# FFN down product of a two-layer hybrid decoder: pairs of row blocks by seven quarter products, weight sums on GpSimd

## The chip, the cores and the metric

The kernel runs on one core of a Trainium2 chip. The metric is the device time of one execution in microseconds, the median of several runs. All arithmetic is on fp32 data; TensorE multiplies operands of type fp32r (fp32 rounded to the shorter form that TensorE takes in one pass).

## The reference, cut to what matters

The trunk has two layers. Each is a half SwiGLU FFN, a token mixing stage (retention, block attention and a convolution side by side), and another half SwiGLU FFN, all with residuals. There are thus four FFNs, and the change touches only their second product. Sequence 256, model width 1024, FFN width 2816.

```python
def swiglu(h, wg, wu, wd):
    return (jax.nn.silu(h @ wg) * (h @ wu)) @ wd
...
    for l in range(DEPTH):
        h = rms_norm(x, ffn1_norm[l])
        x = x + FFN_RES_WEIGHT * swiglu(h, ffn1_wg[l], ffn1_wu[l], ffn1_wd[l])
```

## The kernel before, in words

**Precision.** Every product of two fp32 matrices is made from halves: each operand is split into hi (ScalarE copies it into fp32r, L145 or L196) and lo (VectorE subtracts hi from the source, L146 or L197). A product is then three matmuls: hi by hi, hi by lo, lo by hi.

**The weight stream.** All weights pass once from HBM in "units", each of up to 128x2048 (1 MB). `stream_setup` (L94) lists the units in the order of their use. `fetch` (L118) issues a unit's DMA on SyncE's queue into one of three "raw" tiles (`RBUFS`). `pump` (L130) splits one half of a unit ("a piece", 128x1024) into a whi and a wlo tile; there are 10 such pairs (`WBUFS`). `take` (L152) hands pieces to the matmuls, `free` (L157) gives a pair back. `tick` (L160), called between groups of matmuls, pumps one piece if a pair is free and moves on the other chains of work.

**An FFN** (L387) has 22 row blocks j of 128 hidden columns. The first two are made by `first_pair`. Each later block is one call of `single` (L423): a gate projection and an up projection of 16 matmuls each (8 of 512 columns at L207, 8 of 256 columns at L208), the gate's in a PSUM bank of the tag "mm", the up's in one of the tag "tr", two banks each. After a projection `joined` (L210) folds the bank: ScalarE copies its upper half (L212) and VectorE adds the lower half (L213); only then may the bank be written again. SiLU (L436), the product with up (L438) and the split of the result into hi and lo follow.

**The second product.** `down` (L442) multiplies row block j (128 hidden columns, for each half t of the sequence) by the weights of its 128 rows: for each t two halves of 512 output columns and three matmuls for each, that is 12 matmuls of 512 columns for a block and 24 for a pair of blocks (L450, L451, L454). They accumulate in the four "acc" banks through the whole FFN. The loop at L459 makes two `single`s and then the `down` of the pair made two steps earlier; one such step is called a period here. The last four blocks (`TAIL`) are done at the end, bank by bank (L478), so that the residual of each bank (L484) and the next norm can start while the other banks are still being summed; the transposes of the normed rows (L354) are put between these matmuls.

**Order.** TensorE's order is the program's own throughout. The other engines are ordered by the scheduler, by priority and readiness in its own model, except where `ordered(True)` fixes the program's order (the first pair, the tail). Each engine then executes its queue strictly in that order, and waits are semaphores.

## Time and profile before

| what | value |
|---|---|
| median of 3 runs | 992.77 us (992.19 to 992.94) |
| profiled execution, its own time | 992.42 us |
| its span, first to last instruction | 990.6 us |
| mean granted TensorE clock | 0.999 of full speed |
| PE busy | 973.7 us, 98% |
| DVE (VectorE) busy | 685.4 us, 69% |
| ACT (ScalarE) busy | 537.9 us, 54% |
| POOL (GpSimd) busy | 64.5 us, 7% |

Time of an execution and span differ by 1.8 us, which lies around the first and last instruction. Busy times are unions of records; records of neighbouring instructions of one engine overlap a little, so a sum of single durations is somewhat larger than the busy time.

### The profile page before, as it was taken

The page shows a single profiled execution, that of the slowest core. Times are in us where ns is not written, and L with a number is a line of the kernel's source. Part 1 is how long each engine was busy: PE and PEld are TensorE (multiplying, and loading weights), DVE is VectorE, ACT ScalarE, POOL GpSimd, SP SyncE. Part 2 cuts the span into 40 slices and gives each one's busy share as a digit, 9 for nine tenths or more (in the row PEclk, how much of TensorE's full clock was granted, in tenths as well). Part 3 has the DMA queues.
Part 4 walks back from the last instruction along what each step waited for, and adds up shares of the span by engine and source line. Part 5 has one row for each costly group of instructions (what it writes and reads, how often), then busy time and mean ns, then how long its engine had stood idle before and what let it go on. Part 6 is the DMA issues. An engine that isn't in the chain of part 4 may idle for free.

```text
span 990.6 us, 13759 instructions
## 1 busy us (share of the span) xinstructions
PE 973.7 (98%) x5312; PEld 849.3 (86%) x5312; DVE 685.4 (69%) x1032; ACT 537.9 (54%) x904; POOL 64.5 (7%) x109
## 2 busy tenths in 40 slices
PE   6999999999999999999999999999999999999997
PEld 4888888898997888888888888888989888888885
DVE  6986566569976866666577656566799677666653
ACT  6755555366554755555465545454665456555542
POOL 1000000021141000000000000002100400000000
PEclk9999999999999999999999999999999999999999
DMA  8965554436441855555546555544545437555511
GB/s 307 341 204 202 181 198 163 144 124 215 169 175 64 298 188 194 187 196 184 198 164 222 189 190 192 185 155 138 190 145 192 144 140 264 174 207 177 204 47 43
DMA packets 28722, 180.69 MB, mean 182 GB/s; under 512 B 3440, under 2 KB 3824, under 8 KB 10480
## 3 DMA queue, kind: packets, MB, share of 16 engines
q1 hardware_dynamic: 27360, 176.07, 51.2%
q10 hardware_dynamic: 1296, 3.74, 1.1%
q8 instruction: 42, 0.69, 0.3%
q14 instruction: 24, 0.20, 0.1%
HBM read 178.74 MB, written 1.05 MB: 181 GB/s over the span
## 4 chain that ended last, share of the span: by engine, by line
PE 93%; DVE 5%; ACT 1%; DMA 1%; issue 1%; SPq 0%; POOLq 0%; POOL 0%; DVEq 0%; ACTq 0%
PE mm L207 15%; PE tr L207 15%; PE acc L451 8%; PE acc L450 8%; PE acc L454 8%; PE tr L208 8%; PE mm L208 8%; PE mm L201 4%; PE mm L202 4%; PE mm L203 4%; DVE wlo L146 2%; DVE ac L698 2%; PE acc L207 1%; PE tr L354 1%; PE acc L641 1%; PE mm L787 1%
## 5 line engine op out<-in xcount | busy, mean ns | idle before, releaser
L146 DVE TENSOR_TENSOR wlo<-raw,whi 128x1024 fp32r<-128x1024 f32 (+2 forms) x348 | 402.9, 1169 | 176.9 <-ACT whi L145 173.2
L145 ACT ACTIVATE whi<-raw 128x1024 fp32r<-128x1024 f32 (+2 forms) x348 | 348.6, 1013 | 224.8 <-PE acc L454 87.7
L207 PE MATMUL tr<-hT,whi 128*128 128x512 f32 x640 | 226.0, 391 | 0.0
L207 PE MATMUL mm<-hT,whi 128*128 128x512 f32 x640 | 225.9, 391 | 0.0
L208 PE MATMUL tr<-hT,wlo 128*128 128x256 f32 x640 | 180.5, 282 | 0.0
L208 PE MATMUL mm<-hT,wlo 128*128 128x256 f32 x640 | 180.4, 282 | 0.0
L207 PEld LDWEIGHTS mm<-hT,whi 128*128 128x128 f32 x640 | 120.1, 188 | 25.9
L207 PEld LDWEIGHTS tr<-hT,whi 128*128 128x128 f32 x640 | 120.1, 188 | 25.2 <-issue 0.2
L450 PE MATMUL acc<-whi,hf 128*128 128x512 f32 x352 | 137.7, 391 | 0.0
L451 PE MATMUL acc<-wlo,hf 128*128 128x512 f32 x352 | 137.2, 390 | 0.0
L208 PEld LDWEIGHTS mm<-hT,wlo 128*128 128x128 f32 x640 | 120.8, 189 | 1.4
L208 PEld LDWEIGHTS tr<-hT,wlo 128*128 128x128 f32 x640 | 121.0, 189 | 0.0
L454 PE MATMUL acc<-whi,hf 128*128 128x512 f32 x352 | 113.6, 389 | 0.0
L201 PE MATMUL mm<-whi,hT 128*128 128x384 f32 (+1 forms) x288 | 107.1, 372 | 0.0
L202 PE MATMUL mm<-wlo,hT 128*128 128x384 f32 (+1 forms) x288 | 101.6, 353 | 0.0
L203 PE MATMUL mm<-whi,hT 128*128 128x384 f32 (+1 forms) x288 | 101.1, 351 | 0.0
L454 PEld LDWEIGHTS acc<-whi,hf 128*128 128x128 f32 x352 | 66.1, 188 | 13.9
L450 PEld LDWEIGHTS acc<-whi,hf 128*128 128x128 f32 x352 | 66.1, 188 | 13.6
L451 PEld LDWEIGHTS acc<-wlo,hf 128*128 128x128 f32 x352 | 66.2, 188 | 12.3
L436 ACT ACTIVATE s<-part 128x256 f32<-128x256 f32 x80 | 33.2, 415 | 78.5 <-DVE part L213 78.4
L213 DVE TENSOR_TENSOR part<-part,tr 128x256 f32<-128x256 f32 x80 | 33.6, 420 | 46.8 <-ACT part L212 46.8
L201 PEld LDWEIGHTS mm<-whi,hT 128*128 128x128 f32 x288 | 54.6, 190 | 5.2 <-issue 1.3
(151 smaller groups left out, 954.6 us busy)
## 6 DMA issues: line engine op xcount, KB each, us to landing
raw<-in_wgb SPq DMA_DIRECT2D x80, 1024.0 KB, 4.9
raw<-in_wd SPq DMA_DIRECT2D x44, 1024.0 KB, 4.9
raw<-in_win SPq DMA_DIRECT2D x28, 768.0 KB, 4.5
raw<-in_wout SPq DMA_DIRECT2D x8, 1024.0 KB, 4.8
raw<-in_wga SPq DMA_DIRECT2D x6, 1024.0 KB, 5.1
raw<-in_wcv SPq DMA_DIRECT2D x4, 1024.0 KB, 4.8
raw<-in_wga SPq DMA_DIRECT2D x8, 256.0 KB, 6.5
g<-in_fgain ACTq DMA_DIRECT2D x3, 512.0 KB, 3.7
```

The costliest lines, as they stand in the source:

```text
L145: nc.scalar.activation(hi[:, c], src, AF.Copy)
L146: nc.vector.tensor_tensor(lo[:, c], src, hi[:, c].bitcast(F32), op=OP.subtract)
L201: mm(out, ah, wh, start=start, stop=False)
L202: mm(out, ah, wl, start=False, stop=False)
L203: mm(out, al, wh, start=False, stop=stop)
L207: mm(out, wh, x, start=start, stop=False)
L208: mm(out[:, :S], wl, x[:, 0], start=False, stop=stop)
L213: self.nc.vector.tensor_tensor(v, lo, ps[:, :S], op=OP.add)
L436: nc.scalar.activation(s, v, AF.Silu)
L450: mm(ys[t][h], hi[:, ts], wh[:, n], start=first, stop=False)
L451: mm(ys[t][h], hi[:, ts], wl[:, n], start=False, stop=False)
L454: mm(ys[t][h], lo[:, ts], wh[:, n], start=False, stop=last)
```

## The change

With two row blocks u = (2u, 2u+1) as the inner dimension, the two halves of the sequence as rows and the two halves of 512 output columns as columns, the product of a pair is a 2 by 2 by 2 block product: eight block products, three matmuls each. After the change the first nine pairs of an FFN (`FAST`) use Strassen's algorithm in the form with 15 sums: seven block products, with four sums of weight blocks, four sums of activation blocks and seven sums of products. The last four row blocks (`TAIL`) stay as they were.

- The four sums of weights (128x512 each) are made in place in the raw tile by GpSimd (`sums`). The unit is split in four parts instead of two pieces: B11 alone (128x512, own tiles `wh`, 2 pairs), then B21 and B22 (128x1024), then, after the sums, T1 and T2, and T3 and T4 (128x1024 each). In the stream the last two parts come after the next unit's pieces.
- The four sums of activations (128x128 each) are made by GpSimd in `paired`; the seven blocks are then split, 128x256 and 128x640, instead of 128x256 twice.
- Six of the products stay in PSUM for the FFN: four in the "acc" banks, two in the "mm" banks. So from block 6 on both projections of `single` use the two "tr" banks. The seventh (number 4) goes to a "tr" bank for each pair and is added to the residual at once by VectorE.
- `combine` forms the sums of products before the tail: one ScalarE copy, eight VectorE instructions of 128x512.
- `WBUFS` is 9, and tile pairs are given back in the order of the stream (`release`). `fetch` is held until the raw tile's earlier unit has had all its parts pumped.
- The host lays the two column halves of the down weights the other way round.

```diff
-WBUFS = 10
+FAST = (FT - TAIL) // 2
+WBUFS = 9
+HBUFS = 2
...
                 for p in range(1, FT // 2):
-                    u += [(a["wgb"][f, 2 * p - 2 + i], 2048) for i in range(2)]
+                    plain(a["wgb"][f, 2 * p - 2], 2048)
                     if p > 1:
-                        u.append((a["wd"][f, p - 2], 2048))
+                        w = add(a["wd"][f, p - 2], 2048)
+                        parts.extend(((w, "b11"), (w, "b2")))
+                    plain(a["wgb"][f, 2 * p - 1], 2048)
+                    if p > 1:
+                        parts.extend(((w, "t12"), (w, "t34")))
...
+    def sums(self, raw):
+        b11, b12, b21, b22 = [raw[:, i * 512:(i + 1) * 512] for i in range(4)]
+        gp = self.nc.gpsimd.tensor_tensor
+        gp(b11, b12, b11, op=OP.subtract)
+        gp(b12, b22, b12, op=OP.subtract)
+        gp(b22, b22, b11, op=OP.subtract)
+        gp(b21, b22, b21, op=OP.subtract)
 
     def pump(self):
...
-        while len(self.raws) < min(u + RBUFS, len(self.units)):
+        u, kind = self.parts[self.nparts]
+        half = kind == "b11"
+        if half and self.nhalves == self.half_free + HBUFS:
+            return False
+        if not half and self.nslots == self.oldest + WBUFS:
+            return False
+        while len(self.raws) < len(self.units) and len(self.raws) <= u + RBUFS - 1:
+            if len(self.raws) >= RBUFS and self.left[len(self.raws) - RBUFS]:
+                break
             self.fetch()
...
+        else:
+            if kind == "t12":
+                src = raw.rearrange("p (b n) -> p b n", b=4)[:, 0::3]
+                self.split(*[x.rearrange("p (b n) -> p b n", b=2) for x in (hi, lo)], src)
+            else:
+                first = {"b11": 0, "b2": 1024, "t34": 512}[kind]
+                self.split(hi, lo, raw[:, first:first + size])
+            if kind == "b2":
+                self.sums(raw)
+            self.quads.setdefault(u, {})[kind] = (hi, lo, self.nslots)
...
+    def release(self, seq):
+        self.freed.add(seq)
+        while self.oldest in self.freed:
+            self.oldest += 1
...
+    def free_quad(self, q):
+        self.half_free += 1
+        for k in ("b2", "t34", "t12"):
+            self.release(q[k][2])
...
+            def paired(u):
+                r = rows.pop(u)
+                a11, a12, s1, s2, s4, a21, a22 = [r[:, i] for i in range(7)]
+                gp = nc.gpsimd.tensor_tensor
+                gp(s1, a21, a22, op=OP.add)
+                gp(a21, a11, a21, op=OP.subtract)
+                gp(s2, s1, a11, op=OP.subtract)
+                gp(s4, a12, s2, op=OP.subtract)
+                last = self.scratch(F32R)
+                self.split(*[last[:, h * 256:(h + 1) * 256].rearrange("p (b s) -> p b s", b=2) for h in range(2)], r[:, 5:7])
+                five = fp.tile([P, 2, 5, P], F32R, tag="five", bufs=3, name=self.name("five"))
+                self.split(five[:, 0], five[:, 1], r[:, 0:5])
...
-                for gu, bank in enumerate((self.mmb, self.trb)):
+                for gu, bank in enumerate((self.mmb if j < 6 else self.trb, self.trb)):
...
+            def fast(u):
+                q = self.take_quad()
...
+                terms = {4: ("A22", "T4"), 1: ("A11", "B11"), 6: ("S2", "T2"), 5: ("S1", "T1"), 7: ("S3", "T3"), 3: ("S4", "B22"), 2: ("A12", "B21")}
                 mm = nc.tensor.matmul
+                for i, (x, y) in terms.items():
+                    if i == 4:
+                        bank = self.trb()
+                    else:
+                        if u == 0:
+                            P_[i] = self.mmb() if i in (3, 7) else self.acc()
+                        bank = P_[i]
...
+                    mm(bank, hi, wh, start=first, stop=False)
+                    mm(bank, hi, wl, start=False, stop=False)
+                    mm(bank, lo, wh, start=False, stop=last)
+                    if i == 4:
+                        xs = self.x[1][:, 512:]
+                        nc.vector.scalar_tensor_tensor(xs, bank, -0.5, xs, op0=OP.mult, op1=OP.add)
+                    if i in (6, 7, 2):
+                        self.tick()
+                self.free_quad(q)
...
+            def combine():
...
+                c1, u2, u4 = tmp(), tmp(), tmp()
+                nc.scalar.activation(c1, P_[1], AF.Copy)
+                nc.vector.tensor_tensor(u2, c1, P_[6], op=OP.add)
+                nc.vector.tensor_tensor(u4, u2, P_[5], op=OP.add)
+                resid(0, 0, u4)
+                resid(0, 1, c1)
+                nc.vector.tensor_tensor(u2, u2, P_[7], op=OP.add)
+                resid(1, 0, P_[5])
+                resid(1, 0, u2)
+                resid(1, 1, u2)
...
                 if p > 1:
-                    for j in (2 * p - 4, 2 * p - 3):
-                        (w,) = self.take(1)
-                        for t in range(NT):
-                            down(j, t, w)
-                            if t == 1:
-                                self.free()
-                            self.tick()
+                    fast(p - 2)
...
             tail = self.take(TAIL)
             self.ordered(True)
+            combine()
             for t in range(NT):
                 for h in range(2):
+                    bank = P_[3 - h] if t == 0 else self.acc()
                     for j in range(FT - TAIL, FT):
-                        down(j, t, tail[j - (FT - TAIL)], (h,))
+                        down(j, bank, t, tail[j - (FT - TAIL)], h, t == 1 and j == FT - TAIL)
                         self.tick()
-                    xs = self.x[t][:, h * 512:(h + 1) * 512]
-                    nc.vector.scalar_tensor_tensor(xs, ys[t][h], 0.5, xs, op0=OP.mult, op1=OP.add)
+                    resid(t, h, bank)
                     nxt.half(t, h)
```

## Rows read from the trace of the kernel before

**Rows 1.** The page, parts 1 and 4: busy times, shares of the chain.

```profile
PE 973.7 (98%) x5312; PEld 849.3 (86%) x5312; DVE 685.4 (69%) x1032; ACT 537.9 (54%) x904; POOL 64.5 (7%) x109
...
PE 93%; DVE 5%; ACT 1%; DMA 1%; issue 1%; SPq 0%; POOLq 0%; POOL 0%; DVEq 0%; ACTq 0%
```

**Rows 2.** Stretches: length, each engine's busy us (instructions), clock, DMA share, GB/s.

```profile
25.00:50.00 25.00, 25.00 (x143) 22.00 (x142) 22.59 (x32) 19.76 (x32) 0.00 (x0) 1.00 0.96 345
50.00:75.00 25.00, 25.00 (x133) 21.54 (x133) 21.33 (x55) 12.80 (x21) 0.27 (x1) 1.00 0.59 195
...
400.00:425.00 25.00, 25.00 (x132) 21.54 (x131) 14.96 (x21) 13.17 (x20) 0.00 (x0) 1.00 0.54 183
```

**Rows 3.** Timeline of SyncE's queue: start us, us, instruction; the same unit three periods apart.

```profile
396.35 0.33 SPq L125 DMA_DIRECT2D raw<-in_wd  x1
...
446.05 0.33 SPq L125 DMA_DIRECT2D raw<-in_wd  x1
```

**Rows 4.** Timeline of PE: a pair's first matmul, and the matmul behind its 24.

```profile
398.98 0.39 PE L450 MATMUL acc<-whi,hf 128*128 128x512 f32 x1
...
404.44 0.40 PE L207 MATMUL mm<-hT,whi 128*128 128x512 f32 x1
```

**Rows 5.** Groups by shape: count, busy us, mean ns, idle before and its releasers.

```profile
L146 DVE TENSOR_TENSOR wlo<-raw,whi 128x1024 fp32r<-128x1024 f32 x284 | 345.9, 1226 | 163.7 <-ACT whi L145 160.0
...
L146 DVE TENSOR_TENSOR wlo<-raw,whi 128x768 fp32r<-128x768 f32 x56 | 52.1, 949 | 13.0 <-ACT whi L145 13.0
...
L213 DVE TENSOR_TENSOR part<-part,tr 128x256 f32<-128x256 f32 x80 | 33.6, 420 | 46.8 <-ACT part L212 46.8
...
L484 DVE SCALAR_TENSOR_TENSOR x<-acc,x 128x512 f32<-128x512 f32 x16 | 11.0, 686 | 14.4 <-PE acc L454 14.4
...
L146 DVE TENSOR_TENSOR wlo<-raw,whi 128x512 fp32r<-128x512 f32 x8 | 5.2, 685 | 0.2 <-ACT whi L145 0.2
```

**Rows 6.** Timelines of POOL and DVE: sums in SBUF, beside each other and alone.

```profile
269.70 1.10 POOL L533 TENSOR_TENSOR w<-w,w 128x384 f32<-128x384 f32 x1 [6.65 <-DVE w L532]
269.85 1.23 DVE L698 SCALAR_TENSOR_TENSOR ac<-u,vec,ac 128x256 f32<-128x256 f32 x1
272.59 0.47 DVE L698 SCALAR_TENSOR_TENSOR ac<-u,vec,ac 128x256 f32<-128x256 f32 x1
...
692.39 0.40 POOL L521 TENSOR_TENSOR w<-r,r 128x96 f32<-128x96 f32 x1
```

**Rows 7.** Timelines of DVE and POOL near 688 us: four splits and a small sum.

```profile
687.62 4.09 DVE L146 TENSOR_TENSOR wlo<-raw,whi 128x768 fp32r<-128x768 f32 x4
688.67 3.29 POOL L519 TENSOR_TENSOR r<-w,pc 128x96 f32<-128x96 f32 x1 [1.79 <-ACT w L513]
```

**Rows 8.** Timeline of one `single`: the gate's last matmul, its bank's readers, the up projection.

```profile
407.11 0.28 PE L208 MATMUL mm<-hT,wlo 128*128 128x256 f32 x1
407.23 0.39 PE L207 MATMUL tr<-hT,whi 128*128 128x512 f32 x1
...
408.27 0.37 ACT L212 ACTIVATE part<-mm 128x256 f32<-128x256 f32 x1
...
409.54 0.41 DVE L213 TENSOR_TENSOR part<-part,mm 128x256 f32<-128x256 f32 x1
...
410.00 0.39 PE L207 MATMUL mm<-hT,whi 128*128 128x512 f32 x1
```

**Rows 9.** Timelines of PE and DVE in an FFN's tail, up to the first transpose.

```profile
487.27 0.39 PE L450 MATMUL acc<-whi,hf 128*128 128x512 f32 x1
...
492.91 0.69 DVE L484 SCALAR_TENSOR_TENSOR x<-acc,x 128x512 f32<-128x512 f32 x1 [1.30 <-PE acc L454]
...
495.44 0.88 DVE L348 TENSOR_SCALAR xr<-xr,r 128x512 f32<-128x512 f32 x2 [1.11 <-POOL r L344]
...
496.11 0.38 PE L354 MATMUL tr<-ident,xr 128*128 128x128 f32 x2
```

**Rows 10.** DMA issues: KB each, median us to landing.

```profile
raw<-in_wd SPq DMA_DIRECT2D x44, 1024.0 KB, 4.9
```

More of the change, by code (lines that the diff above doesn't have):

```diff
@@ L95, in stream_setup, with add, plain @@
         a = self.a
-        u = []
+        u, parts = [], []
+        def add(src, n):
+            u.append((src, n))
+            return len(u) - 1
+        def plain(src, n):
+            i = add(src, n)
+            parts.extend((i, h) for h in range(2))
         for l in range(L):
@@ L150, in pump @@
+        self.nparts += 1
+        self.left[u] -= 1
+        if half:
+            self.nhalves += 1
+        else:
+            self.nslots += 1
         return True
@@ L456, in ffn, with down @@
+            def down(j, bank, t, w, h, first):
+                hi, lo = [x[:, t * P:(t + 1) * P] for x in hf[j]]
+                wh, wl = [x[:, (1 - h) * 512:(2 - h) * 512] for x in w]
+                mm = nc.tensor.matmul
+                mm(bank, hi, wh, start=first, stop=False)
+                mm(bank, hi, wl, start=False, stop=False)
+                mm(bank, lo, wh, start=False, stop=j == FT - 1)
             first_pair()
```

145 lines of the change are left out of this document (92 added, 53 removed).

## The prediction

> **What bounds the kernel now.** I read the page first. TensorE is busy for 98% of the span and holds 93% of the chain of waits [rows 1], so the kernel is bound by TensorE. An edit gains only what it takes off TensorE's queue, and loses whatever makes TensorE wait. The windows show how much the others have in hand: in the middle of an FFN VectorE is busy 14.96 of 25 us, ScalarE 13.17, GpSimd not at all; in the first 50 us VectorE is busy 22.59 and 21.33 of 25, and TensorE still 25.00 [rows 2]. A VectorE that is 90% busy can thus be hidden here. The queue of SyncE gives the rhythm: the same unit is fetched 49.70 us and three periods later, so a period takes 16.57 us [rows 3]. In it the 24 matmuls of a pair take 404.44 - 398.98 = 5.46 us, that is 0.2275 us each [rows 4]; the rest, 11.1 us, are two `single`s.
>
> **What leaves TensorE.** Seven block products of three matmuls replace eight: 21 instead of 24 for a pair, nine pairs in each of four FFNs. That is 3 x 36 = 108 matmuls of 0.2275 us [rows 4], **-24.6 us**. The period would fall to 16.57 - 0.68 = 15.89 us. Nothing is added to TensorE's queue: the sums go elsewhere, and the order of blocks inside a pair costs nothing, since each matmul already loads its own stationary block.
>
> **What goes to VectorE and ScalarE.** Durations are mean records [rows 5]. Before, a period has six splits of 1.226 us, four folds, two products and two splits of 128x256 (eight of about 0.42): 10.7 us. The window says 14.96 / 25 x 16.57 = 9.9 us [rows 2], because neighbouring records overlap; I scale by 9.9 / 10.7 = 0.93. After it there are four plain splits (4.90), the pair's unit in four parts (0.685 + 3 x 1.226 = 4.36), four folds, two products and the 128x256 split (7 x 0.42 = 2.94), the 128x640 split (between 0.42 and 0.949, the latter being the 768-column row; in proportion 0.82), and the residual of product 4 from PSUM (0.69, as the row of 0.686). That sums to 13.7 us, scaled 12.7 us. In 15.89 us this is 80%, less than the 90% that the start of the kernel hides. ScalarE gets the same parts: it was at 13.17 of 25 us, and with 384 more activation columns and 1536 more weight columns a period, at no more than VectorE's time for them (2.4 us), it stays near 70%. I cost both at nothing as mere work; the cover is TensorE's 15.89 us, and it is gone if VectorE's total passes that.
>
> **What goes to GpSimd, and what it takes from VectorE.** Eight sums a period. A sum of two SBUF operands takes 1.10 us for 384 columns and 0.40 us for 96 [rows 6]; in proportion 1.41 for 512 and 0.48 for 128, so 4 x 1.41 + 4 x 0.48 = 7.6 us of 15.89. GpSimd itself is far from full. But the same rows show a price: a VectorE instruction with two SBUF operands takes 0.47 us alone and 1.23 us beside the 1.10 us sum [rows 6], so it stood still for 0.76 us. Scaled by columns a 512-column sum can hold VectorE up for 1.02 us and a 128-column sum for 0.25: at most 4 x 1.02 + 4 x 0.25 = 5.1 us a period. It can also go the other way: beside four splits in a row, which took 4.09 us, a 96-column sum took 3.29 us instead of 0.40 [rows 7]; then VectorE loses nothing and the sum comes 2.9 us late. The lower bound is therefore 0, the upper 5.1, and VectorE's period lies between 12.7 and 17.8 us. I take half, 2.55: the folds and product 4 read PSUM, and in a fifth of the time VectorE has nothing to do. With 15.3 us against 15.89, TensorE stays the bound, narrowly.
>
> The Trainium skill (SBUF — State Buffer, section "Who interferes with whom") says that VectorE with two SBUF inputs and GpSimd reading SBUF exclude each other, and that whoever comes second is fully blocked for the whole instruction. The trace agrees that they exclude each other, but the row has 0.76 us of 1.10; by the rule at its word, 7.6 us a period, VectorE would need up to 20.3 us and the kernel about 1127 us.
>
> **The bank wait.** From block 6 on both projections share two "tr" banks, so a gate bank is wanted again after one projection, 2.77 us (407.23 to 410.00); before, it was wanted after two. Today the gate's last matmul ends at 407.39, ScalarE copies at 408.27 and VectorE ends its addition at 409.95 [rows 8]: 2.56 us. That leaves 0.21 us. The delay is the weight split that either engine is in the middle of. Two gates a period meet this; a weight sum is under way in about 5.6 of 15.89 us, so I let one of the two meet one, and take half of its 1.02 us, 0.51. TensorE then waits 0.51 - 0.21 = 0.30 us in each of 4 x 8 periods: **+9.6 us**. The ends are 0 and one whole sum at both gates, 2 x (1.02 - 0.21) x 32 = 52 us; the value is nearer to the lower end because the latency already contains a full split in the way. The wait of product 4 for the second gate's bank is the second of the two; its own VectorE read has almost seven microseconds before that bank is next written.
>
> **The tail.** `combine` puts eight VectorE instructions of 0.69 us ahead of the residuals, 5.5 us. Their inputs are ready up to 2.7 us before the tail begins, as product 2 and product 3 come last; so they end 3 to 5.5 us into it. Today the second residual begins 492.91 - 487.27 = 5.64 us into the tail, and the first transpose starts at 496.11, while the scaling before it runs from 495.44 [rows 9]: no slack to speak of. The first residual and norm step (two of 0.69) must now fit behind `combine`; I take a delay of 0.5 us for each FFN, **+2 us**, with ends 0 and 1.3 each. The four tail pieces still find tile pairs: five slots of the last pair and four make nine, so `WBUFS` at 9 costs nothing there.
>
> **The start.** From 50 to 75 us VectorE also makes the position tables and is at 85% [rows 2]; 2.8 us of new work and 2.55 of standing still in 15.89 us bring it to 119% for about one period: **+3 us**, ends 0 and 6.
>
> **The sum.** -24.6 + 9.6 + 2 + 3 = -10.0 us. From the profiled execution's own 992.42 us (span 990.6 and 1.8 around it; the median of the runs, 992.77, is 0.04% above it) that gives **982.4 us**. With the bank wait between 4 and 16 us, this case's own range is 976 to 989.
>
> **The rivals.**
> *All of it is hidden.* The scheduler puts the folds ahead of the splits and VectorE's free fifth takes up the sums. For it: TensorE at 25.00 of 25 with VectorE at 22.59 [rows 2]. Against it: 0.21 us of slack at the bank [rows 8]. Only the tail's low end remains: 992.4 - 24.6 + 1.2 = 969 us.
> *Saving and waits cancel.* The bank wait is 0.6 us instead of 0.3 a period: about 992 us.
> *The shared operand path becomes the bound* (slower). VectorE passes TensorE once its losses exceed 15.89 - 12.7 = 3.2 us a period; from 16.57 - 12.7 = 3.9 of the 5.1 us, 76%, the kernel is slower than before. For it: the row shows nearly full exclusion [rows 6]; two-operand splits are most of VectorE's time, so a sum will nearly always meet one. Against it: VectorE's instructions can go first [rows 7]. Between 76% and 100% I take 4.5 us: 17.2 us a period, 36 x 0.63 + 5 for tail and start = +28, 1020 us.
> *The pair's unit comes late* (slower). Its raw tile is held from landing to the last part: 4.9 us of transfer [rows 10], 1.9 us for the first two parts, 5.6 us for the sums, 2.5 us for the last two: 14.9 us if nothing waits, and 19.8 us if each sum waits for one split of 1.23 us [rows 5, 7]. If the next such unit needs this tile, a period of 15.89 us doesn't hold that; ScalarE, whose queue is strict, then stands before the late part with the folds behind it. At the middle, 17.3 us, it gives about 1018 us. Against it: a raw tile is free earlier, from the unit in between.
>
> **Chances.** Forecast 0.40, all hidden 0.17, cancel 0.09, shared path 0.22, late unit 0.12. Faster by over 0.2% (2 us, about what a measurement of this kernel can tell from no change) is 0.40 + 0.17 = 0.57, the same 0.09, slower 0.34. The range from 968 to 1012 us takes in the first three cases and the lower part of both slower ones (a loss of 4.2 us a period rather than 4.5); about 0.2 is left out, nearly all above.
>
> **What would show it.** Right: 108 fewer matmuls of 512 columns; VectorE at about 80% to 95% in the middle of an FFN; TensorE's new waits short, at the first matmul of a projection or of product 4, ended by VectorE's fold; VectorE's two-operand records lengthened by up to 1 us beside GpSimd's sums. The period read from SyncE's queue should be about 16.2 us. Wrong: a period of 15.9 with no waits (all hidden); VectorE near 100% and TensorE waiting for weight parts (shared path); ScalarE idle before a part that GpSimd releases, or before a landing (late unit); a gap of several us at the transposes after `combine`.

## The result, and the profile after

The changed kernel takes **1165.2 us** (median of 4 runs, 1164.4 to 1166.2), the kernel before 992.9 us in the same comparison (4 runs): ratio **1.173**, 95% interval 1.172 to 1.175. The forecast was 982.4 us with a range up to 1012, so the sign was wrong and the result lies far outside the range. In line numbers of the kernel after, a split is L277 (ScalarE) and L278 (VectorE), a fold is L293 (ScalarE's copy) and L294 (VectorE's addition), GpSimd's weight sums are L164 to L167, its activation sums L484 to L487, and the products are L576 to L578.

The page after, parts 1 and 4, beside [rows 1]:

```profile
PE 1013.2 (87%) x5204; PEld 862.8 (74%) x5204; DVE 898.5 (77%) x1172; ACT 599.4 (52%) x988; POOL 422.6 (36%) x397
...
DVE 32%; PE 30%; issue 15%; POOL 8%; ACT 8%; DMA 6%; SPq 0%; POOLq 0%; DVEq 0%; ACTq 0%
```

The 108 matmuls are gone (5312 to 5204), and yet TensorE is busy for 39.5 us more (1013.2 against 973.7) and idle for 133.2 us more (1163.3 - 1013.2 = 150.1, before 990.6 - 973.7 = 16.9). TensorE's share of the chain falls from 93% to 30%. No engine is full: the kernel is bound by waits that go round from engine to engine.

Two stretches in the middle of an FFN, beside [rows 2], and SyncE's queue, beside [rows 3]:

```profile
500.00:525.00 25.00, 21.29 (x105) 17.79 (x103) 20.07 (x23) 13.77 (x21) 11.07 (x9) 0.93 0.47 167
525.00:550.00 25.00, 21.20 (x112) 17.98 (x113) 20.08 (x22) 13.81 (x22) 14.84 (x12) 1.00 0.48 170
```

```profile
492.44 0.33 SPq L154 DMA_DIRECT2D raw<-in_wd  x1
512.33 0.33 SPq L154 DMA_DIRECT2D raw<-in_wd  x1
```

VectorE is at 80%, as forecast, and TensorE at 85%. A period takes 512.33 - 492.44 = **19.9 us**; it was 16.57, and the forecast said about 16.2.

What TensorE waits for, and then what ScalarE waits for (total us, times, longest us):

```profile
PE tr L288 <- DVE part L294: 68.6, 30, 5.4
PE tr L576 <- DVE part L294: 39.2, 21, 6.3
PE tr L435 <- DVE xr L429: 22.2, 4, 9.4
```

```profile
ACT hf L277 <- POOL rows L485: 84.9, 34, 4.3
ACT whi L277 <- PE tr L288: 58.5, 30, 3.0
ACT five L277 <- POOL rows L487: 28.4, 34, 1.4
```

The new waits have the ends that the forecast named, VectorE's fold ahead of a projection (L288) and of product 4 (L576). But there are 107.8 us of them, and ScalarE stands 113.3 us for GpSimd's activation sums. Of the third wait, 9.4 us lie at the kernel's start, where before has 9.2; the other 12.8 are at the ends of the first three FFNs.

By stretches, from the first seven-product matmul of an FFN to its last matmul, and from there to the next FFN's first: the FFNs take 190.1, 184.3, 184.0 and 177.8 us (before 150.0, 150.0, 150.0, 149.0: **+137.2**), the passages between them 163.5, 38.2 and 163.6 (before 151.1, 34.7, 151.1: **+28.4**; the first and third hold a mix stage), the start is 6.9 us later, the end 0.1. But for rounding that is the 172.7 us by which the spans differ.

Groups by shape on VectorE and then on GpSimd, beside [rows 5, 6]:

```profile
L278 DVE TENSOR_TENSOR wlo<-raw,whi 128x1024 fp32r<-128x1024 f32 x320 | 443.2, 1410 | 38.5 <-ACT whi L277 34.9
...
L543 DVE TENSOR_TENSOR rows<-s,part 128x256 f32<-128x256 f32 x64 | 49.0, 766 | 0.8
```

```profile
L167 POOL TENSOR_TENSOR raw<-raw 128x512 f32<-128x512 f32 x36 | 73.1, 2029 | 2.6
...
L484 POOL TENSOR_TENSOR rows<-rows 128x128 f32<-128x128 f32 x36 | 43.5, 1209 | 129.5 <-DVE rows L543 129.5
```

A large split takes 1.41 us instead of 1.23, the product of gate and up projection 0.77 instead of 0.42. The sums on GpSimd took longer than I had scaled: 1.4 to 2.0 us for 512 columns (forecast 1.41), 1.21 for the first of the 128-column sums (forecast 0.48). Those that VectorE did not disturb took 1.29 and 0.46 us (526.16 and 516.27 us), so the scaling held and the rest is VectorE in the way.

One period shows how these add up. First the wait on TensorE, then the queues of GpSimd, ScalarE and VectorE in the same time (the last rows of GpSimd and VectorE are of the period's later part):

```profile
522.80 0.39 PE L288 MATMUL tr<-hT,whi 128*128 128x512 f32 x1
...
525.34 0.50 PE L288 MATMUL tr<-hT,whi 128*128 128x512 f32 x1 [2.03 <-DVE part L294]
```

```profile
514.82 1.38 POOL L484 TENSOR_TENSOR rows<-rows 128x128 f32<-128x128 f32 x1 [3.61 <-DVE rows L543]
516.27 0.46 POOL L485 TENSOR_TENSOR rows<-rows 128x128 f32<-128x128 f32 x1
516.69 0.46 POOL L486 TENSOR_TENSOR rows<-rows 128x128 f32<-128x128 f32 x1
517.23 0.73 POOL L487 TENSOR_TENSOR rows<-rows 128x128 f32<-128x128 f32 x1
...
534.74 1.38 POOL L484 TENSOR_TENSOR rows<-rows 128x128 f32<-128x128 f32 x1 [3.60 <-DVE rows L543]
```

```profile
516.77 0.42 ACT L277 ACTIVATE hf<-rows 128x256 fp32r<-128x256 f32 x1 [2.46 <-POOL rows L485]
517.99 0.74 ACT L277 ACTIVATE five<-rows 128x640 fp32r<-128x640 f32 x1 [0.81 <-POOL rows L487]
518.64 2.94 ACT L277 ACTIVATE whi<-raw 128x1024 fp32r<-128x1024 f32 x3
521.48 0.61 ACT L277 ACTIVATE whhi<-raw 128x512 fp32r<-128x512 f32 x1
522.00 1.05 ACT L277 ACTIVATE whi<-raw 128x1024 fp32r<-128x1024 f32 x1
522.95 0.36 ACT L293 ACTIVATE part<-tr 128x256 f32<-128x256 f32 x1
```

```profile
519.72 3.50 DVE L278 TENSOR_TENSOR wlo<-raw,whi 128x1024 fp32r<-128x1024 f32 x3
523.13 0.68 DVE L278 TENSOR_TENSOR whlo<-raw,whhi 128x512 fp32r<-128x512 f32 x1
523.73 1.22 DVE L278 TENSOR_TENSOR wlo<-raw,whi 128x1024 fp32r<-128x1024 f32 x1
524.87 0.41 DVE L294 TENSOR_TENSOR part<-part,tr 128x256 f32<-128x256 f32 x1
...
527.66 4.55 DVE L278 TENSOR_TENSOR wlo<-raw,whi 128x1024 fp32r<-128x1024 f32 x2
532.14 0.41 DVE L294 TENSOR_TENSOR part<-part,tr 128x256 f32<-128x256 f32 x1
```

The gate's matmuls end at about 520.4 us. Its fold ends at 525.3, 4.9 us later (before: 2.56 [rows 8]), because both engines take their queues in order and the fold stands behind five weight splits. These stand behind the splits of the activation blocks, and those wait for GpSimd, whose first sum was held up by a split of VectorE (1.38 us where the next take 0.46). TensorE then waits 2.03 us, later in the same period 1.45 us for product 4's bank: that fold (532.14) stands behind two weight splits which took 4.55 us beside the weight sums instead of 2 x 1.23. The second block's product follows, and with it the next activation sums, which start at 534.74, 19.92 us after 514.82. The loop is closed and its length is the period, so a delay anywhere in it lengthens every period.

At the end of an FFN (start of the first transposes, then a 4 us stretch with its granted clock), beside [rows 9]:

```profile
240.54 1.08 PE L435 MATMUL tr<-ident,xr 128*128 128x128 f32 x4 [3.73 <-DVE xr L429]
```

```profile
240.00:244.00 4.00, 3.46 (x13) 3.05 (x14) 1.59 (x4) 1.41 (x4) 0.22 (x1) 0.57 0.00 2
```

The transposes wait 3.73 us, and behind the wait the granted clock is 0.57, so it is at the lower of its two levels (1.2 GHz) for most of this stretch. This recurs behind many of the waits and makes the clock's mean 0.951.

### The profile page after: what moved, and what is told of

Read it like the earlier page. It is cut to its first block, busy times and chain, and to the rows that moved or that the text cites. A ratio compares the mean times of both kernels' runs of the same rounds, so it can differ in the third digit from the quotient of the medians.

```text
span 1163.3 us, 14178 instructions
## 1 busy us (share of the span) xinstructions
PE 1013.2 (87%) x5204; PEld 862.8 (74%) x5204; DVE 898.5 (77%) x1172; ACT 599.4 (52%) x988; POOL 422.6 (36%) x397
## 4 chain that ended last, share of the span: by engine, by line
DVE 32%; PE 30%; issue 15%; POOL 8%; ACT 8%; DMA 6%; SPq 0%; POOLq 0%; DVEq 0%; ACTq 0%
DVE wlo L278 18%; PE tr L288 6%; DMA raw<-in_wd 5%; ACT whi L277 5%; DVE part L294 3%; PE tr L289 3%; PE mm L282 3%; PE mm L283 3%; PE mm L284 3%; POOL rows L484 3%; DVE whlo L278 2%; POOL rows L487 2%; DVE ac L849 2%; DVE rows L543 1%; PE acc L288 1%
## 5 line engine op out<-in xcount | busy, mean ns | idle before, releaser
L278 DVE TENSOR_TENSOR wlo<-raw,whi 128x1024 fp32r<-128x1024 f32 (+2 forms) x384 | 500.4, 1330 | 40.8 <-ACT whi L277 37.2
L288 PE MATMUL tr<-hT,whi 128*128 128x512 f32 x1152 | 433.7, 414 | 68.8 <-DVE part L294 68.6
L277 ACT ACTIVATE whi<-raw 128x1024 fp32r<-128x1024 f32 (+2 forms) x384 | 377.9, 1012 | 109.3 <-PE tr L288 58.5
L289 PE MATMUL tr<-hT,wlo 128*128 128x256 f32 x1152 | 335.9, 292 | 0.0
L288 PEld LDWEIGHTS tr<-hT,whi 128*128 128x128 f32 x1152 | 228.9, 199 | 129.6 <-DVE part L294 79.9
L289 PEld LDWEIGHTS tr<-hT,wlo 128*128 128x128 f32 x1152 | 230.4, 200 | 1.2
L164 POOL TENSOR_TENSOR raw<-raw 128x512 f32<-128x512 f32 x36 | 71.6, 1989 | 211.9 <-DVE whlo L278 191.5
L538 ACT ACTIVATE s<-part 128x256 f32<-128x256 f32 x80 | 33.3, 416 | 145.1 <-DVE part L294 145.1
L294 DVE TENSOR_TENSOR part<-part,tr 128x256 f32<-128x256 f32 x144 | 59.9, 416 | 57.6 <-ACT part L293 57.6
L484 POOL TENSOR_TENSOR rows<-rows 128x128 f32<-128x128 f32 x36 | 43.5, 1209 | 129.5 <-DVE rows L543 129.5
L167 POOL TENSOR_TENSOR raw<-raw 128x512 f32<-128x512 f32 x36 | 73.1, 2029 | 2.6
L293 ACT ACTIVATE part<-tr 128x256 f32<-128x256 f32 x144 | 52.6, 365 | 15.5 <-PE tr L289 15.5
L277 ACT ACTIVATE hf<-rows 128x256 fp32r<-128x256 f32 x36 | 15.0, 418 | 85.0 <-POOL rows L485 84.9
L282 PEld LDWEIGHTS mm<-whi,hT 128*128 128x128 f32 x288 | 54.6, 189 | 5.2 <-issue 1.3
L278 DVE TENSOR_TENSOR five<-rows,five 128x640 fp32r<-128x640 f32 x36 | 34.0, 944 | 31.0 <-ACT five L277 31.0
L278 DVE TENSOR_TENSOR hf<-rows,hf 128x256 fp32r<-128x256 f32 x36 | 18.5, 513 | 50.4 <-ACT hf L277 50.4
L283 PEld LDWEIGHTS mm<-wlo,hT 128*128 128x128 f32 x288 | 54.7, 190 | 3.6 <-DVE wlo L278 1.3
L284 PEld LDWEIGHTS mm<-whi,hT 128*128 128x128 f32 x288 | 54.4, 189 | 3.1 <-DVE hT L278 0.3
```

The costliest lines, as they stand in the source:

```text
L164: gp(b11, b12, b11, op=OP.subtract)
L167: gp(b21, b22, b21, op=OP.subtract)
L277: self.nc.scalar.activation(hi, src, AF.Copy)
L278: self.nc.vector.tensor_tensor(lo, src, hi.bitcast(F32), op=OP.subtract)
L282: mm(out, ah, wh, start=start, stop=False)
L283: mm(out, ah, wl, start=False, stop=False)
```

## The experiments

Times are medians where a ratio with its interval stands beside them, otherwise the time of a single execution; the kernel before took 992.0 to 993.0 us beside them. "Period" is read from SyncE's queue or from the starts of the seven products.

### The bank, and the order of the queues

**Products 7 and 3 in the banks of 5 and 6**, so that the gates have their "mm" banks back. This kernel leaves out that these products are kept apart.

```diff
-                for gu, bank in enumerate((self.mmb if j < 6 else self.trb, self.trb)):
+                for gu, bank in enumerate((self.mmb, self.trb)):
...
-                            P_[i] = self.mmb() if i in (3, 7) else self.acc()
+                            P_[i] = P_[{7: 5, 3: 6}[i]] if i in (3, 7) else self.acc()
...
```

> The changed kernel, but products 7 and 3 are summed into the banks of products 5 and 6, so that the two 'mm' banks stay with the gate projections as before the change; left out is only that these products are kept apart. All work of VectorE, ScalarE and GpSimd stays. Bank theory (TensorE waits because a fold stands behind splits in strict queues and the two 'tr' banks are wanted again after 2.77 us): the 2.0 and 1.5 us waits of a period go, 19.92 falls to 16 to 16.7 us, about 1020 to 1050 us in all. Port theory (GpSimd's sums take VectorE's second operand path, so VectorE is the bound): the period stays above 19 us, about 1150 us, and the waits move to other places.

Measured: 1141.9 us, 23.3 less than the change, and the period is mostly still 19.9. The waits for a projection's bank have gone, those of product 4 have grown from 39.2 to 85.6 us. The shared bank is where most of the delay shows, not what makes it.

**The kernel before with both projections in the two "tr" banks** from block 6 on, and nothing else of the change.

```diff
-                for gu, bank in enumerate((self.mmb, self.trb)):
+                for gu, bank in enumerate((self.mmb if j < 6 else self.trb, self.trb)):
```

> The kernel before, with both projections of every block from number 6 on in the two 'tr' banks (the two 'mm' banks idle), nothing else changed. If the shared banks alone are the cost: two waits of a us or more a period as in the changed kernel, above 1050 us. If they cost only together with late queues: the fold's 2.56 us against the 2.77 us available, no wait or up to 0.3 us a period: 993 to 1003 us.

Measured: 999.2 us, 6.4 more than before (992.8). TensorE's weight loads wait 6.0 us for folds in 29 places. This is what sharing costs without any sum in the way. The 9.6 us of the forecast were for folds that meet a sum, so that the two numbers are near each other supports nothing.

**The program's own order on all engines** (`ordered` left out), **activation splits two ticks later**, and **tile pairs given back in any order**:

```diff
-            self.ordered(False)
...
-            self.ordered(True)
```

> The changed kernel with the program's order on all engines through the whole FFN (the scheduler's freedom is taken away), so that a fold stands behind the parts pumped before the end of its projection and not behind five splits. Queue theory: the waits at the 'tr' banks shrink to below 1 us each, period 16.5 to 18 us, 1010 to 1095 us. Port theory: VectorE still loses 2.5 us a period and the period stays above 19 us. If waits for GpSimd in a strict queue are what costs, it gets worse than 1165 us, since the program's order puts the activation splits right behind the sums.

```diff
+                yield 2
                 last = self.scratch(F32R)
...
-                            paired(j // 2)
+                            self.spawn(paired(j // 2))
...
```

> The changed kernel with the two activation splits of a pair issued two ticks after their sums instead of at once. Theory of the late activation sums: ScalarE's 3.3 us and VectorE's 2.5 us of idle time before these splits go and the period falls as with the sums on VectorE, to 18 to 18.5 us, 1090 to 1110 us. If the free scheduler puts the splits at the same place anyway, the order is the same and the time within 10 us of 1165 us.

```diff
-        if not half and self.nslots == self.oldest + WBUFS:
+        if not half and self.nslots - self.nfreed == WBUFS:
...
```

> The changed kernel, but a tile pair counts as given back as soon as its block products are done, and not only once all older ones are (the pump's limit is the number of pairs in use). Bunch theory (five pairs come back at once at the end of a pair's 21 matmuls, so five splits stand in a row before the fold): the splits are spread, the 2.0 us wait halves or goes, period 18 to 19 us, 1090 to 1125 us. Queue and port theory: no more than 0.3 us a period, 1150 to 1170 us.

Measured: 1275.1, 1166.2 and 1155.2 us. The program's order is worse, for the activation splits then follow straight on the sums, and ScalarE stands 210.1 us for them in place of 84.9 (at L485); issuing them two ticks later leaves ScalarE's waits as they were (84.2 us); the third takes 3.5 to 4.2 us off each of the first three FFNs, behind their last pair, and the periods stay at 19.9.

### GpSimd: results that come late, and the operand path

**No weight sums** (the parts are split without them).

```diff
-            if kind == "b2":
-                self.sums(raw)
```

> The changed kernel without the four sums of weights (the blocks are split as they lie; the products are of unsummed blocks). Port theory: VectorE gets back the 1.1 us that each blocked split of 1024 columns loses (2.29 instead of 1.22 us), some 2 us a period: period about 17.7 us, 1085 us in all. Bank theory: the folds are still behind the splits of the queue, the first wait (2.0 us) stays and the second (1.5 us) goes: about 18.4 us a period, 1110 us. Theory of the late activation sums (ScalarE and VectorE stand before splits that wait for GpSimd's activation sums): 19 us or more, the idle time before these splits is unchanged.

**Activation sums on VectorE**, weight sums on GpSimd.

```diff
-                gp = nc.gpsimd.tensor_tensor
+                gp = nc.vector.tensor_tensor
```

> The changed kernel with the four sums of activations on VectorE instead of GpSimd. Theory of the late activation sums: the 2.5 us of VectorE's idle time and the 3.3 us of ScalarE's before these splits go, the queues come to the next folds earlier, the wait of 2.0 us goes: period about 17.5 to 18 us, 1075 to 1095 us. Port theory: little, the large sums are still there: 1140 to 1165 us. Bank theory alone: within 20 us of the changed kernel, as the order of folds and splits is unchanged.

Measured: 1107.6 us with periods of 18.3 and 19.9, and 1104.5 us with 18.3. Either half of GpSimd's work suffices for a period of 18 us and more: the activation sums by their place in the loop, the weight sums, for which ScalarE waits only 12.1 us in all, mainly by stretching VectorE's instructions (the last run below).

**All eight sums on VectorE**, none on GpSimd.

```diff
-        gp = self.nc.gpsimd.tensor_tensor
+        gp = self.nc.vector.tensor_tensor
...
-                gp = nc.gpsimd.tensor_tensor
+                gp = nc.vector.tensor_tensor
```

> The changed kernel with all eight sums of a period on VectorE, none on GpSimd. Port theory: the lengthened records (2.3 instead of 1.22 us for a split) go; VectorE has 12.7 + 4 x 0.6 + 4 x 0.3 = 16.3 us of plain work a period, the period falls to 16.5 to 17.5 us, 1010 to 1050 us in all. Queue theory (the first gate's fold stands behind five splits, and these behind the activation splits; the loop fold, second block, its product, activation sums, five splits, fold is the period): the 18.3 us of the run with the activation sums on VectorE, with 1.1 to 2.2 us given back by the port and 2.4 us of weight sums put into the same queue: 18 to 19 us, 1090 to 1125 us.

Measured: 1011.1 us, one stretch in the middle of an FFN:

```profile
400.00:425.00 25.00, 25.00 (x139) 21.87 (x139) 24.75 (x38) 15.18 (x25) 0.00 (x0) 1.00 0.65 230
```

TensorE is at 25.00 of 25 us and the period is **15.9 us**, the 15.89 of the forecast. VectorE does 24.75 of 25 and TensorE does not wait for it: an engine at 99% can be hidden, GpSimd at 44 to 59% was not. But the time is still above that of before.

**The kernel before with four GpSimd sums of 128x512 per down-weight unit that nobody waits for**: the operand path alone.

```diff
...
         self.ready.append((hi, lo))
+        if i == 0 and u in self.down_units:
+            gp = self.nc.gpsimd.tensor_tensor
+            for k in range(4):
+                gp(self.junk, raw[:, 512 * (k % 4):512 * (k % 4) + 512], raw[:, 512 * ((k + 1) % 4):512 * ((k + 1) % 4) + 512], op=OP.subtract)
```

> The kernel before with four additional GpSimd sums of 128x512 for each unit of the down weights, from the raw tile into a tile that nobody reads: the use of the operand path without anyone waiting for a sum. Port theory: VectorE's splits beside them are lengthened by about 1 us (1.22 to 2.3), 2 to 4 us a period; VectorE at 60% takes up most of it, and the time rises by 0 to 40 us. Theory of late sums (waits for GpSimd's results are what costs): no more than 5 us.

Measured: 996.1 us, 3.6 more. Its page, part 1, and its large splits:

```profile
PE 974.8 (98%) x5312; PEld 849.3 (85%) x5312; DVE 791.0 (80%) x1032; ACT 532.0 (54%) x904; POOL 378.2 (38%) x285
```

```profile
L149 DVE TENSOR_TENSOR wlo<-raw,whi 128x1024 fp32r<-128x1024 f32 x284 | 420.0, 1492 | 73.0 <-ACT whi L148 69.1
```

VectorE's busy time grows by 791.0 - 685.4 = 105.6 us for 176 sums, 0.60 us each, and TensorE hardly notices: its periods stay at 16.57 us. The stretching costs little in this kernel, whose gates have banks of their own; that it costs as little in the changed one doesn't follow (the last run below).

### What is left without GpSimd

In the run with all sums on VectorE the mix passages take 158.7 us (before 151.1). I took this first for VectorE's backlog at the end of an FFN.

**The last four operations of `combine` after the first half of the norm**, on top of it.

```diff
...
-            combine()
+            u2 = combine()
             for t in range(NT):
+                if t == 1:
+                    combine_late(u2)
```

> All eight sums of a period on VectorE, as in the run of 1011 us, and the last four VectorE instructions of the sums of products (those for the second half of the sequence) moved behind the norm of the first half. Tail theory (between the last pair of an FFN and the next stage the run loses some 7 to 14 us, since VectorE does eight sums and four tail splits before the first residual): 2.8 us come off the chain before the first transposes, and with it the TensorE clock's fall there: 3 to 6 us for each of four FFNs, 985 to 1000 us in all. If something else holds the transposes: within 3 us of 1011.

Measured: 1008.7 us (ratio 1.0155, 1.0138 to 1.0172). The FFNs get shorter (148.7, 148.6, 147.4, 143.1), the mix passages longer (163.0 and 162.7).

**Seven products in the last FFN alone**, then **in FFNs 1 and 3**; the others as in the kernel before.

```diff
...
-                self.ffn(2 * l + 1, s[2], s[3])
+                (self.ffn if 2 * l + 1 in FAST_FFNS else self.ffn_plain)(2 * l + 1, s[2], s[3])
...
```

> Seven products in the last FFN alone (FFN 3, after which no other stage follows), all its eight sums on VectorE, the last four operations of the combination after the first half of the norm; FFNs 0 to 2 as in the kernel before. Theory (the period of 15.89 us is real, and the sums on VectorE lose it again only where a next stage waits for rows, transposes and weights): nine periods of 0.68 us less are 6.1 us, the combination at the very end gives back 1 to 4 us, so 988 to 991 us, below the kernel before. Rival (VectorE, full in this FFN, is late within it too, at its first units, or the combination at the end costs as much as the periods give): 993 us or more.

> Seven products in FFNs 1 and 3, the others as in the kernel before. After FFN 1 an FFN follows and no mix stage; in the run with all sums on VectorE in all FFNs that passage took 7.5 us longer than in the kernel before, and with the late combination 4.7 us. Theory: FFN 1 gains 6.1 us and loses about 5 at that passage, so 987 to 990 us, within 1.5 us of the kernel with FFN 3 alone. Rival (the loss at a passage is that of a full VectorE whatever follows): FFN 1 loses more than it gains, and the time is 2 us or more above that of the kernel with FFN 3 alone.

Measured: 1007.6 us (ratio 1.0150, 1.0136 to 1.0164) and 1009.2 (1.0159, 1.0138 to 1.0180): a miss that showed where to look. FFN 3 takes 143.9 us instead of 149.0, as the theory had it. The loss is in the two mix passages (159.4 and 158.6 us), whose code is that of before and which follow FFNs of before. What remains different there is the weight tile pairs: 9 instead of 10, given back in the order of the stream. The 1.6 us between the two runs lie within the spread of either (1005.1 to 1011.4 us) and say nothing about FFN 1's end.

**The kernel before with 9 pairs:**

```diff
-WBUFS = 10
+WBUFS = 9
```

> The kernel before with 9 pairs of weight tiles in place of 10, and nothing else. Theory (the tenth pair is what the mix stages need: in the run with seven products in FFN 3 alone, the two mix stages, whose code is that of before, took 159.4 and 158.6 us from the last product of one FFN to the first of the next, before 151.1): 7 to 8 us per mix stage, so 1006 to 1010 us, and no change inside the FFNs (150.0 us each). Rival (the order in which tile pairs are given back or the sums do it): 993 to 995 us.

Measured: **1012.5 us** (ratio 1.0204, 1.0178 to 1.0230), more than expected: the passages take 163.7 and 160.0 us, the FFNs 150 as ever. Its waits on TensorE, then one of them on ScalarE's side:

```profile
211.42 0.50 PE L207 MATMUL acc<-hT,whi 128*128 128x512 f32 x1 [1.03 <-ACT whi L145]
212.68 0.39 PE L208 MATMUL acc<-hT,wlo 128*128 128x256 f32 x1 [0.76 <-DVE wlo L146]
218.14 0.50 PE L207 MATMUL acc<-hT,whi 128*128 128x512 f32 x1 [0.74 <-ACT whi L145]
```

```profile
210.31 1.06 ACT L145 ACTIVATE whi<-raw 128x1024 fp32r<-128x1024 f32 x1 [1.79 <-PE acc L207]
```

The mix stage holds so many pairs that with nine the next piece is split only when a product ends, and the next product starts only when the piece is split. TensorE is also busy for 10.0 us longer with the same 5312 matmuls (983.7 against 973.7), at a mean granted clock of 0.992 against 0.999, so about half of the 20 us are not waits.

**Ten pairs, with the memory of nine pairs and two halves**: b11 takes a whole pair, pairs are given back in any order; sums on VectorE, late combination. First with seven products in FFN 3 alone, then in all four.

```diff
-WBUFS = 9
+WBUFS = 10
...
-        if half and self.nhalves == self.half_free + HBUFS:
-            return False
-        if not half and self.nslots == self.oldest + WBUFS:
+        if self.nslots - self.nfreed == WBUFS:
...
-        for k in ("b2", "t34", "t12"):
+        for k in ("b11", "b2", "t34", "t12"):
...
```

> Seven products in FFN 3 alone, sums on VectorE, 10 pairs of weight tiles given back in any order; the block b11 takes a whole pair in place of a half-sized one, so the memory is that of 9 pairs and 2 halves. Theory: the mix stages take 151 us again; FFN 3 keeps 143.9 us against 149.0 (so in the run with 9 pairs), the end after the last product takes 8.0 us against 6.6: 992.9 - 5.1 + 1.4 = 989 us, 988 to 990. Rival (whole pairs for b11 leave FFN 3 without lead): FFN 3 takes 147 us or more, 992 us or more.

> The same in all four FFNs: seven products, sums on VectorE, late combination, 10 pairs of weight tiles. From the run with 9 pairs: FFNs 148.7, 148.6, 147.4 and 143.1 us against 150.0, 150.0, 150.0 and 149.0, 11 us less; passages 163.0, 35.5 and 162.7 against 151.1, 34.7 and 151.1; start 2.8 and end 1.4 us later. Theory (7.5 to 8.3 us of each mix passage are the tenth pair): 992 to 996 us. Rival (VectorE's lack of lead makes these passages, whatever the number of pairs): passages stay above 160 us, 1005 us or more.

Measured: **988.7 us** (ratio 0.9961, 0.9949 to 0.9973) and **988.6 us** (0.9966, 0.9954 to 0.9978): both below the kernel before. With FFN 3 alone the passages are at 151.1 us again. With all four, the FFNs take 150.2, 148.0, 145.1 and 143.9 us, the passages 154.9, 38.3 and 153.5.

**Seven products in FFNs 2 and 3**, chosen from these stretches.

> Seven products in FFNs 2 and 3, the other two as in the kernel before; sums on VectorE, late combination, 10 pairs. From the run with all four: FFN 2 takes 145.1 us against 150.0, the passage after it 153.5 against 151.1, FFN 3 143.9 against 149.0, the end 1.4 us more; FFNs 0 and 1 gained 0 and 2.0 us there and lost 3.8 and 3.6 at their passages. Theory: 992.3 - 4.9 + 2.4 - 5.1 + 1.4 = 986 us, 985 to 988. Rival (FFN 2 gained there from what FFN 1 left behind): FFN 2 takes 147 us or more, 988.5 us or more.

Measured: **986.3 us** (0.9936, 0.9922 to 0.9949), the fastest kernel here, 6.7 us below before. Its page, parts 1 and 4, and its waits on TensorE:

```profile
PE 963.9 (98%) x5258; PEld 838.7 (85%) x5258; DVE 790.6 (80%) x1246; ACT 573.5 (58%) x946; POOL 64.2 (7%) x109
...
PE 90%; DVE 7%; ACT 1%; issue 1%; DMA 1%; SPq 0%; POOL 0%; POOLq 0%; ACTq 0%; DVEq 0%
```

```profile
PE tr L440 <- DVE xr L434: 8.0, 1, 8.0
PE mm L287 <- ACT hT L282: 2.9, 2, 1.7
```

54 fewer matmuls, 9.8 us less TensorE work, and no matmul waits for a fold; the first wait is that of the kernel's start, the second lies at the passages. FFN 2 takes 145.0 us, FFN 3 144.0, the passage between them 153.5.

**The change's own sums on GpSimd, with ten pairs**; then **the weight sums alone on GpSimd, with ten pairs** (this one with the late combination).

> The changed kernel with all its sums on GpSimd as they are, and 10 pairs of weight tiles given back in any order, b11 in a whole pair. Theory (the loss has two parts: the mix passages, which the tenth pair takes back, and the period of 19.9 us, which the results from GpSimd and the operand path make): the mix passages fall from 163.5 us towards 152 to 156, the periods stay at 19.5 us or more, so 1140 to 1152 us. Rival (the tenth pair also gives the periods their lead, and GpSimd's sums then cost nothing): periods below 17 us, under 1050 us.

> Seven products in all FFNs, weight sums on GpSimd, activation sums on VectorE, late combination, 10 pairs of weight tiles; against the run with 10 pairs and all sums on VectorE (988.6 us) only the 144 weight sums move to GpSimd. Theory (with 9 pairs the period of 18.3 us was VectorE filled by splits that GpSimd's operands stretch, and a full engine is not helped by a tenth pair): the period stays at 17.5 us or more and the time at 1050 us or more. Rival (it was the lead of the nine pairs): the period falls to 16.3 us or less, and the time to 1010 us or less, since VectorE is relieved of 36 x 4 sums.

Measured: 1095.1 us (ratio 1.1029, 1.1009 to 1.1049) and 1054.1 (1.0619, 1.0601 to 1.0637). SyncE's queue of the first and of the second:

```profile
626.15 0.33 SPq L154 DMA_DIRECT2D raw<-in_wd  x1
644.12 0.33 SPq L154 DMA_DIRECT2D raw<-in_wd  x1
```

```profile
626.97 0.33 SPq L154 DMA_DIRECT2D raw<-in_wd  x1
644.03 0.33 SPq L154 DMA_DIRECT2D raw<-in_wd  x1
```

The periods are 18.0 and 17.1 us. The first is a miss: I had expected the tenth pair to help the passages only, and it takes 1.9 us off every period too. ScalarE's queue of that run says how:

```profile
455.39 2.94 ACT L272 ACTIVATE whi<-raw 128x1024 fp32r<-128x1024 f32 x3
458.23 0.36 ACT L288 ACTIVATE part<-tr 128x256 f32<-128x256 f32 x1
```

Three splits stand between the activation blocks and the fold, not five. In the second run the time is as expected, the period a little lower than expected, and VectorE is busy 21.98 of 25 us from 420 to 445 us, not full: TensorE waits 27.2 us for folds ahead of product 4 and 14.8 ahead of projections, again behind stretched splits. One of them, with the GpSimd sum beside it:

```profile
637.99 1.35 POOL L166 TENSOR_TENSOR raw<-raw 128x512 f32<-128x512 f32 x1
638.13 2.29 DVE L273 TENSOR_TENSOR wlo<-raw,whi 128x1024 fp32r<-128x1024 f32 x1
640.35 0.41 DVE L289 TENSOR_TENSOR part<-part,tr 128x256 f32<-128x256 f32 x1
...
640.81 0.50 PE L571 MATMUL tr<-whi,hf 128*128 128x512 f32 x1 [0.62 <-DVE part L289]
```

ScalarE waits only 1.6 us for weight sums in this whole run, and 13.6 us for landings of weights (29.5 with all sums on VectorE and ten pairs). So what they cost here is not that they come late: they lengthen the splits that stand ahead of a fold.

The steps, each against the one above it (the last two rows are without the late combination, worth 1011.1 - 1008.7 = 2.4 us between the two runs with nine pairs that differ in it). The period is that of the middle of an FFN; the stretches are those of the profiled executions, which took 992.4, 992.3, 1048.4, 1098.6 and 1165.4 us:

| Kernel | Time, us | Period, us | Four FFNs, us | Two mix passages, us |
|---|---|---|---|---|
| before | 992.8 | 16.57 | 599.0 | 302.2 |
| all sums on VectorE, ten pairs | 988.6 | about 16.0 | 587.2 | 308.4 |
| weight sums on GpSimd, ten pairs | 1054.1 | 17.1 | 641.9 | 308.5 |
| all sums on GpSimd, ten pairs | 1095.1 | 18.0 | 684.7 | 312.4 |
| the change: all on GpSimd, nine pairs | 1165.2 | 19.9 | 736.2 | 327.1 |

In this order the weight sums on GpSimd cost 65.5 us, the activation sums, with `combine` in one piece again, 41.0 and the lack of the tenth pair 70.1. Another order divides the loss otherwise: with nine pairs, leaving out the weight sums gave back 57.6 us, moving the activation sums to VectorE 60.8, and moving all sums there 154.1, more than the two together.

## Why the prediction was wrong

**What leaves TensorE: right.** 108 matmuls fewer, and a period of 15.9 us wherever nothing makes TensorE wait.

**VectorE's and ScalarE's plain work: right within 5% for VectorE.** In the run with all sums on VectorE it is busy 24.75 / 25 x 15.89 = 15.7 us a period; the eight sums among it are 4 x 0.69 + 4 x 0.29 = 3.9 us, or 3.6 with the forecast's factor of 0.93, which leaves 12.1 against 12.7. ScalarE is busy 15.18 of 25 us there, 61%, where I had said near 70%.

**What GpSimd takes from VectorE: right in size, not in what it costs.** Against the same instructions in that run, the large splits cost 443.2 - 386.2 = 57.0 us more, the products 49.0 - 27.0 = 22.0, the two activation splits 7.6: 86.6 us over 36 periods, 2.4 a period (forecast 2.55; no row stood behind the half that I took of the upper bound, so part of this is luck). The Trainium skill (SBUF — State Buffer, section "Who interferes with whom") has the second of the two blocked for the whole instruction, and the order of issue deciding which. The trace agrees that both sides block: with the idle sums VectorE lost 0.60 us a sum, while the sums took 1.78 us, not the 1.29 of an undisturbed one at 526.16 us in the kernel after. The 1127 us that I worked out from the rule rested on a VectorE that is full; at 80% it is not, so that 1127 is nearer to 1165 than my forecast doesn't support it. But I let the 2.4 us vanish in VectorE's free fifth, and they don't: with ten pairs the weight sums alone cost 65.5 us, while VectorE has room.

**The cover: the step that failed.** I counted GpSimd's 7.6 us and VectorE's 15.3 us against 15.89, called GpSimd "far from full", and took what fits under 15.89 as hidden, but for 0.30 us a period at the banks. Nobody waits for an engine's load, though; they wait for its results, and those come when their turn in a strict queue has come. ScalarE waits 113.3 us for GpSimd's activation sums, for whose coming late my sum had no term, with everything in its queue behind it; and the folds come late behind VectorE's stretched splits. The loop of these waits, 19.92 us, took the place of TensorE's 15.89. The rival of the late unit named the sign (ScalarE idle before a part that GpSimd releases), for the weight parts; it was the activation blocks.

**The bank wait: the same failure seen from TensorE.** I took 0.30 us a period, for one weight split and perhaps one sum ahead of the fold. Measured are 110.0 us of waits for folds, 3.1 a period, with five splits ahead, themselves behind a wait for GpSimd. The kernel before with two banks (+6.4 us) and the change with its own banks (23.3 us less, periods still 19.9) show that sharing the banks is a small part of the 172 us.

**Nine tile pairs: "costs nothing" failed.** I looked at the FFN's tail only, where it holds; the mix stages, which I didn't look at since the diff leaves them alone, need the tenth. That costs the kernel before 20 us, and with GpSimd in the loop 70 us, most of it in the periods, which are 19.9 instead of 18.0 (1165.2 - 1095.1; giving back in any order, about 10 in the run that did only that, is part of it).

**Tail and start: too low.** The gap of several us at the transposes behind `combine`, which I had named as a sign of being wrong, is there (3.73 us), and it lies inside the FFN's stretch. So the whole end is read from the first matmul of FFN 1's last pair of seven products to the first such matmul of FFN 2: 62.2 us (568.98 to 631.21) instead of 52.1 (481.82 to 533.89). An FFN's end thus costs about 10 us here, not 0.5. It is 59.6 us with all sums on VectorE, and 56.7 with ten pairs and the late combination as well, so most of it is not GpSimd's; `combine` and VectorE's backlog are what is left, and no run parts them. The start is 6.9 us late, not 3.

**The clock: no term at all.** For the same 5204 matmuls TensorE is busy 1013.2 us here and 960.6 with ten pairs and no GpSimd: 52.6 us, which came as stretches at 1.2 GHz behind the waits (mean granted clock 0.951 against 0.994).

Not settled: how much of the 65.5 us comes with the other order that the scheduler gives the queues there, how the 41 us between the last two ten-pair rows divide between the activation sums' latency and their share of the operand path, how the 70 us of the tenth pair divide between the pair and the order of giving back, and whether another order of the queues would let GpSimd's sums stay. The program's own order and the later activation splits did not.

## What to carry to other kernels

An engine with free time is not a free engine: before work goes to it, follow its result to the first instruction that waits for it, and count what is queued behind that instruction on a strict queue; do the same for each instruction of a neighbour that the new work stretches; if the path comes back to its own start, its length sets the period. A buffer taken away is priced in the stage that holds the most of them, which need not be one that the change touches. And a gain that drowns in side costs can be had by undoing these one at a time: seven products pay here with the sums on VectorE, with ten pairs, and in the last two FFNs, which gain more inside (5.0 us each) than their ends lose (2.4 and 1.3).

## What I had not expected of the hardware

VectorE at 24.75 of 25 us cost TensorE nothing in the middle of an FFN, while VectorE at 20.07 of 25 with GpSimd beside it left TensorE idle for 15% of the time.

Waits of about 2 us did not all do the same to the clock: in the stretch from 505 to 510 us, with a wait of 2.02 us before its 505.45, the granted clock is 0.67; from 525 to 530 us, with the wait of 2.03 us before 525.34, it is 1.00. So the cost of a short wait could not be read from its length alone.
